# Modulation weights through a buffer and a queue of their own, and decay constants computed earlier, in a two-block decoder kernel

## The chip, the cores and the metric

The kernel runs on one core of a Trainium2 chip, as one launch. The metric is the device time of that launch in microseconds. Three runs of the kernel before took 985.2, 986.3 and 988.33 us; the median is 986.3 us. Engines are named as the profile names them: PE (matmul) with PEld (its weight loads), DVE, ACT, POOL (GpSimd) and SP, which issues most of the DMAs.

## The reference

There are 256 tokens of width 1024, all in float32. The first block mixes three attention branches (a low-rank attention with rotary positions, a dilated attention in three groups, and attention over 256 memory rows), gates each with a sigmoid of its own projection, adds them, and runs a convolutional feed-forward network of width 2816. The second block has two layers. Each layer modulates its input with a shift, a scale and a gate that depend on a condition vector `c`, and runs a gated linear recurrence beside a matrix-memory branch:

```
c_act = silu(c)
for l in range(2):
    mod = c_act @ w_ada[l] + b_ada[l]            # 1024 -> 3072
    shift, scale, gate = split(mod, 3)
    h = rms_norm(x, norm_g[l]) * (1 + scale) + shift
    ...                                          # h @ w_in, both branches, y = [..] @ w_out
    # in the recurrence: log_a = -8 * r * softplus(-lam)
    x = x + gate * y
```

The modulation depends on `c` alone, so it can be computed at any time before the second block. So can `softplus(-lam)`, which depends on a parameter alone.

## The kernel before

**Products.** Each float32 weight block of 128x1024 (512 KB) is fetched by SP into one of four buffers of the pool `raw`. ACT rounds it to `hi` (L254), DVE subtracts to get `lo` (L257), and PE forms three products for each pair (L266). The helper `load` does this for all weights, and `hi` and `lo` have four buffers each. A block that takes part in a product with 256 columns gives PE 24 matmuls. A `raw` buffer is free for the next fetch when its subtraction has ended, and SP issues in its own order, so a fetch that waits for a buffer holds back all that stand behind it.

**Modulation.** `w_ada` has 24 blocks of 128x1024 for each layer, 48 in all. A block is not multiplied on PE: DVE forms the dot product of each row with `c_act` in one pass (L504, a multiplication with an accumulator, in two records: the pass and the reading of the accumulator) and writes a column of `mod`. The generator `ada_blocks` yields after each block; `ada_steps(n)` takes n steps of it. In the kernel before, a step fetches a block through the same four `raw` buffers and the same SP queue (L503) and reduces it at once.

**The order.** The string `MIX` lists the steps of the mixing stage: `ls`, `lt`, `ly` are scores, transposes and sums of one head of the low-rank attention, `ds`, `dt`, `dy` those of the dilated one, `dp` a projection for it, `ga` to `gc` and `ba` to `bc` gates and branches, and `x1`, `x2`, `x3` are one, two or three modulation steps. There are 28 modulation steps in it, 9 more in the output projection and the feed-forward's down projection, and 13 in the first layer. From the program so recorded a scheduler sets the order of the instructions on each engine; what it builds is fixed then, and each engine runs its instructions in that order, waiting at each for its semaphores.

**Decay constants.** `csp` and `ncsp` (128x16) are computed by 2 activations on ACT and 25 short DVE operations and a memset (L987 to L1001), written in the program behind the feed-forward network.

**POOL** has little to do before: it adds in the feed-forward network (L948), issues nine DMAs, among them `ali` (768 KB, the bias of the dilated attention, twice) and `row` (512 KB, a gain spread over the partitions), and masks and adds in the second block.

Of the kernel before, what the change touches and what calls it, by code (L numbers as in the profile page):

```python
# [28 lines left out]
FENCE = 4  # L29
STREAM = 32  # L30
HOLD = 3
MIX = """gc0 lr ms0 gc1 ln ms1 mt0 gc2 my0 ms2 mt1 lq0 my1 lq1 ms3 mt2 lq2 my2 lq3 mt3 lk my3 lv gc3
    ls0 bc0 bc1 ls1 bc2 bc3 lt0 dp0 ly0 ls2 lt1 x1 dp1 ly1 ls3 lt2 x1 dp2 ly2 ls4 lt3 x1 dp3 ly3 ls5 lt4 x1 dp4 ly4 ls6 lt5 x1 dp5 ly5 ls7 lt6 x1 dp7 ly6 lt7 x1 ga0 ly7 x1 dp6 x1
    x1 ga1 x1 ga2 x1 ds0 ga3 ds1 ba0 ba1 ba2 ba3 dt0 dp8 dy0 dt1 dp9 dy1 x1 dp10 x2 dp11 x2 dp12 x2 dp13 x2 dp14 x3 ds2 dp15 x1
    ds3 gb0 x1 dt2 gb1 x1 dy2 x1 dt3 gb2 dy3 gb3 bb0 bb1 bb2 bb3"""
ADA_O = ((1,), (1,), (1,), ())
ADA_DOWN = ((1, 4), (3,), (1, 4), (1,))
ADA_RGZ = (1, 1, 1, 1)
# [159 lines left out]
def block_kernel(ctx: ExitStack, tc: tile.TileContext, T: dict, out: bass.AP):  # L198
    nc = tc.nc
    pe, act, dve, pool, dma = nc.tensor, nc.scalar, nc.vector, nc.gpsimd, nc.sync  # L200

    cp = ctx.enter_context(tc.tile_pool(name="cp", bufs=1))
    rawp = ctx.enter_context(tc.tile_pool(name="rawp", bufs=RAW))
# [7 lines left out]
    fill2 = ctx.enter_context(tc.tile_pool(name="fill2", bufs=1))  # L211
    dve.memset(fill2.tile([P, 48], F32, name="fill2"), 0.0)
# [10 lines left out]

    def slot(i, dt=F32, stream=False):
        a = STREAM if stream else 0
        return sp.tile([P, KT * S + 64], dt, name=f"s{i}", tag=f"s{i}")[:, a:a + KT * S].rearrange("p (k n) -> p k n", k=KT)
# [102 lines left out]
    def col(name, i=0, n=1):  # L329
        return cols[:, COL[name] + i:COL[name] + i + n]  # L330
# [19 lines left out]
    dve.memset(cp.tile([P, STREAM], F32, name="fill3"), 0.0)  # L350
# [11 lines left out]
    class Sums:  # L362
# [6 lines left out]
        def add(self, sq, k):  # L369

            if k < 6:
                g = k % 4
                pe.matmul(self.part[32 * g:32 * g + 32], lhsT=ones[:, :32], rhs=sq, start=k < 4, stop=k >= 2)
            if k == 5:
                part = one()
                act.copy(part, self.part)
                self.out = [sm_tile()[:, :P], sm_tile()[:, :P]]
                for t in range(2):
                    pe.matmul(self.out[t], lhsT=part[:, t * P:(t + 1) * P], rhs=ones32, start=True, stop=False)
# [118 lines left out]
    mod = cp.tile([P, 2, 24], F32, name="mod")  # L498

    def ada_blocks(l, c_act):  # L500
        for m in range(24):
            raw = rawp.tile([P, 1024], F32, name="raw", tag="raw")
            dma.dma_start(out=raw, in_=T[f"w_ada{l}"][m])  # L503
            dve.tensor_tensor_reduce(out=raw, in0=raw, in1=c_act, op0=ALU.mult, op1=ALU.add, scale=1.0,  # L504
                                     scalar=0.0, accum_out=mod[:, l, m:m + 1])
            yield
        dve.tensor_tensor(out=mod[:, l], in0=mod[:, l], in1=col("b_ada_2", 24 * l, 24), op=ALU.add)
        dve.scalar_tensor_tensor(out=mod[:, l, 8:16], in0=mod[:, l, 8:16], scalar=1.0, in1=col("norm_g_2", 8 * l, 8),
                                 op0=ALU.add, op1=ALU.mult)
        while True:  # L510
            yield
# [11 lines left out]


    with tc.tile_pool(name="l1", bufs=1) as l1, tc.tile_pool(name="pS", bufs=1) as pS:
        dve.memset(l1.tile([P, STREAM], F32, name="fill5"), 0.0)
        mask = l1.tile([P, S], F32, name="mask")
        yT = l1.tile([P, 8, S], F32R, name="y", tag="y")

# [62 lines left out]
        for quarter in (0.0, 0.25):  # L592
# [4 lines left out]
            r = one()  # L597
# [33 lines left out]
        rs_kv = t2.tile([P, S], F32, name="rstd", tag="rstd", bufs=3)  # L631

        rcs = {}

# [173 lines left out]
        def merge_branch(name, j, tg, first=False):  # L808
# [4 lines left out]
            else:  # L813
                t = two()
                dve.scalar_tensor_tensor(out=t, in0=tg[:, jj], scalar=1.0, in1=ps, op0=ALU.add, op1=ALU.mult)
                dve.tensor_tensor(out=merged[:, jj], in0=merged[:, jj], in1=t, op=ALU.add)


        sx, pts, yps, sets, tgs, ali = {}, {}, {}, {}, {}, {}
        for step in MIX.split():  # L820
            n, i = step.rstrip("0123456789"), int(step.lstrip("abcdefghijklmnopqrstuvwxyz_") or 0)
            if n == "ms":
                sx[n, i] = mem_scores(i)
            elif n == "mt":
                pts[n, i] = transposed(sx["ms", i], [0, S, P, S + P])
            elif n == "lt":
                pts[n, i] = transposed(sx["ls", i], [S, 0, P])
            elif n == "dt":
                pts[n, i] = transposed(sx["ds", i], [768, 896, 1024, 0, 128, 256, 384, 512, 640])
            elif n == "my":  # L830
                mem_sums(i, pts["mt", i])
            elif n == "lr":
                mla_sums_of_squares()
            elif n == "ln":
                mla_norms()
            elif n == "lq":
                mla_q(i)
            elif n == "lk":
                mla_k()
            elif n == "lv":  # L840
                mla_v()
            elif n == "ls":
                sx[n, i] = mla_scores(i)
            elif n == "ly":
                if i % 2 == 0:
                    yps[i // 2] = sm_tile()
                mla_sums(i, pts["lt", i], yps[i // 2])
            elif n == "dp":
                p = i // 8
                if i % 8 == 0:  # L850
                    sets[p] = [slot(x) for x in ((6, 4, 5), (0, 1, 2))[p]]
                dil_proj(p, i % 8, sets[p])
            elif n == "ds":
                if i % 2 == 0:
                    ali[i // 2] = dil_bias(i // 2)
                sx[n, i] = dil_scores(i % 2, sets[i // 2], ali[i // 2])
            elif n == "dy":
                dil_sums(i // 2, i % 2, sets[i // 2], pts["dt", i])
            elif n in ("ga", "gb", "gc"):
                if i == 0:  # L860
# [117 lines left out]

    for l in range(2):
        pool.dma_start(out=wif[:, l], in_=T[f"w_if{l}"])  # L980


    lam = col("rg_lambda_2", 0, 16)
    csp = l2.tile([P, 16], F32, name="csp")
    ncsp = l2.tile([P, 16], F32, name="ncsp")
    e, f, z2, w = (l2.tile([P, 16], F32, name=n) for n in ("sp_e", "sp_f", "sp_z", "sp_w"))
    act.activation(e, lam, AF.Abs)  # L987
    act.activation(e, e, AF.Exp, scale=-1.0)
    dve.tensor_scalar(out=f, in0=e, scalar1=2.0, scalar2=None, op0=ALU.add)
    dve.reciprocal(f, f)  # L990
    dve.tensor_tensor(out=f, in0=e, in1=f, op=ALU.mult)
    dve.tensor_tensor(out=z2, in0=f, in1=f, op=ALU.mult)
    dve.memset(w, 1.0 / 17.0)
    for k in (15, 13, 11, 9, 7, 5, 3, 1):
        dve.tensor_tensor(out=w, in0=w, in1=z2, op=ALU.mult)
        dve.tensor_scalar(out=w, in0=w, scalar1=1.0 / k, scalar2=None, op0=ALU.add)
    dve.tensor_tensor(out=w, in0=w, in1=f, op=ALU.mult)
    dve.tensor_scalar(out=e, in0=lam, scalar1=-1.0, scalar2=0.0, op0=ALU.mult, op1=ALU.max)
    dve.scalar_tensor_tensor(out=csp, in0=w, scalar=2.0, in1=e, op0=ALU.mult, op1=ALU.add)
    dve.tensor_scalar(out=csp, in0=csp, scalar1=4.0, scalar2=None, op0=ALU.mult)  # L1000
    dve.tensor_scalar(out=ncsp, in0=csp, scalar1=-1.0, scalar2=None, op0=ALU.mult)  # L1001

    def conv4(dst, ps, l, wname, bname, j):
        for m in range(2):
# [351 lines left out]
```

## Time and profile before

| | |
|---|---|
| median of 3 runs | 986.3 us |
| the profiled execution: its time, its span | 987.47 us, 985.8 us |
| busy: PE, DVE, ACT, POOL | 953.3, 735.2, 626.7, 53.8 us |
| mean clock granted to PE, as a share of full speed | 0.995 |
| weights fetched by SP | 185.17 MB |
| DMAs of POOL | 4.33 MB |
| modulation blocks | 48 of 512 KB, 59.3 us of DVE |

A matmul's end is modelled, so PE's busy time holds its short stalls only where they are longer than the pipeline is deep. Idle time before an instruction is shown in brackets with what ended it. The sum of a prediction is made against the span and its 987.47 us; the median lies 1.2 us lower.

### The profile page before, as it was taken

The numbers are of one execution on the slowest core, as the hardware profiler recorded it, in microseconds if no ns is written. First come the engines' busy times: TensorE is split into PE (matmuls) and PEld (weight loads), VectorE is DVE, ScalarE is ACT, GpSimd is POOL, SyncE is SP. The second block draws the span as 40 slices with busy tenths as digits, with TensorE's granted clock in tenths as the row PEclk, the third lists the DMA queues.
The fourth block names the chain that finished last, engine by engine and source line by source line (L and its number), as shares of the span: only waits on it lengthen the run. The fifth ranks groups of instructions, "written<-read, shape, count | busy, mean of one in ns | idle before, by whom it ended". The sixth has DMA issues, their size and how long they took to land.

```text
span 985.8 us, 19651 instructions
## 1 busy us (share of the span) xinstructions
PE 953.3 (97%) x7880; PEld 916.2 (93%) x7880; DVE 735.2 (75%) x1281; ACT 626.7 (64%) x1042; POOL 53.8 (5%) x61
## 2 busy tenths in 40 slices
PE   7999999999999999999989999999999999999997
PEld 5999999899989989999989899898999998899997
DVE  5856766567565888888856788589986798687754
ACT  7666555454345578887744776895645677886643
POOL 0000000000000002111200000000001000000021
PEclk9999999999999999999999999999999999999999
DMA  8654576777786766565667365355786464345552
GB/s 300 212 177 129 176 230 209 249 235 225 250 252 205 224 194 205 183 197 186 204 219 240 126 210 163 120 170 162 250 268 219 131 209 152 108 128 193 172 177 80
DMA packets 53371, 190.74 MB, mean 193 GB/s; under 512 B 6080, under 2 KB 6464, under 8 KB 53280
## 3 DMA queue, kind: packets, MB, share of 16 engines
q1 hardware_dynamic: 52272, 185.17, 58.0%
q0 software_dynamic: 1008, 4.33, 1.4%
q8 instruction: 61, 1.00, 0.4%
q14 instruction: 30, 0.25, 0.1%
HBM read 188.42 MB, written 1.05 MB: 192 GB/s over the span
## 4 chain that ended last, share of the span: by engine, by line
PE 66%; DVE 12%; ACT 10%; DMA 7%; issue 4%; POOL 0%; DVEq 0%; SPq 0%; ACTq 0%; POOLq 0%
PE mm L266 56%; DVE lo L257 5%; DMA raw<-in_w_ada 5%; ACT hi L254 3%; ACT fz L945 2%; ACT fw L946 2%; DVE fu L939 1%; PE sm L1051 1%; ACT s L491 1%; DMA raw<-in_w_dv 1%; DVE raw L504 1%; PE sm L1256 1%; PE sm L1207 1%; PE sm L669 1%; DMA raw<-in_w_mlx 1%
## 5 line engine op out<-in xcount | busy, mean ns | idle before, releaser
L257 DVE TENSOR_TENSOR lo<-raw,hi 128x1024 fp32r<-128x1024 f32 (+2 forms) x300 | 369.6, 1244 | 95.6 <-ACT hi L254 93.8
L254 ACT CAST hi<-raw 128x1024 fp32r<-128x1024 f32 (+2 forms) x300 | 308.7, 1040 | 153.0 <-PE mm L266 80.1
L266 PE MATMUL mm<-H,hi 128*128 128x256 f32 x1456 | 236.9, 281 | 0.1
L266 PE MATMUL mm<-H,lo 128*128 128x256 f32 x1456 | 233.4, 278 | 1.4 <-DVE lo L257 1.4
L266 PE MATMUL mm<-L,hi 128*128 128x256 f32 x1456 | 234.2, 279 | 0.1
L266 PEld LDWEIGHTS mm<-H,hi 128*128 128x128 f32 x1456 | 197.6, 189 | 2.2 <-DVE s L1008 0.8
L266 PEld LDWEIGHTS mm<-H,lo 128*128 128x128 f32 x1456 | 197.6, 189 | 1.6 <-DVE lo L257 1.6
L266 PEld LDWEIGHTS mm<-L,hi 128*128 128x128 f32 x1456 | 197.7, 189 | 0.7 <-DVE L L1029 0.3
L266 PE MATMUL mm<-hi,s 128*128 128x256 f32 (+1 forms) x1032 | 148.0, 283 | 0.2 <-ACT s L494 0.2
L266 PEld LDWEIGHTS mm<-hi,s 128*128 128x128 f32 x1032 | 131.8, 189 | 1.9 <-ACT s L494 0.4
L504 DVE CUSTOM_DVE_ANT_0 raw<-raw,c_act 128x1024 f32<-128x1024 f32 x48 | 59.3, 1235 | 63.4 <-DMA raw<-in_w_ada 63.4
L266 PE MATMUL mm<-lo,s 128*128 128x256 f32 (+1 forms) x516 | 84.9, 284 | 5.7 <-DVE lo L257 5.7
L266 PEld LDWEIGHTS mm<-lo,s 128*128 128x128 f32 x516 | 70.5, 190 | 7.0 <-DVE lo L257 6.1
L266 PE MATMUL mm<-s,hi 128*128 128x256 f32 x320 | 53.5, 286 | 0.0
L266 PEld LDWEIGHTS mm<-s,hi 128*128 128x128 f32 x320 | 44.3, 190 | 6.3 <-PE mm L266 2.5
L438 ACT ACTIVATE sq<-xn 128x256 f32<-128x256 f32 (+1 forms) x28 | 14.3, 511 | 43.6 <-POOL xn L1320 32.6
L266 PE MATMUL mm<-s,lo 128*128 128x256 f32 x160 | 34.2, 281 | 0.0
L945 ACT ACTIVATE fz<-fu,cols 128x256 f32<-128x256 f32 x44 | 26.2, 595 | 7.6 <-DVE fu L939 7.6
L948 POOL TENSOR_TENSOR fz<-fz,fw 128x508 f32<-128x508 f32 x22 | 24.7, 1125 | 109.1 <-DVE fz L947 109.1
L491 ACT CAST s<-two 128x512 fp32r<-128x512 f32 x24 | 14.9, 619 | 22.7 <-DVE two L1261 22.7
L657 ACT ACTIVATE sx<-sx,nm 128x256 f32<-128x256 f32 (+3 forms) x24 | 13.3, 555 | 24.6 <-DVE nm L654 24.6
L266 PEld LDWEIGHTS mm<-s,lo 128*128 128x128 f32 x160 | 25.4, 189 | 2.0 <-issue 1.2
(320 smaller groups left out, 1152.1 us busy)
## 6 DMA issues: line engine op xcount, KB each, us to landing
raw<-in_w_ada SPq DMA_DIRECT2D x48, 512.0 KB, 4.5
raw<-in_w_up SPq DMA_DIRECT2D x44, 512.0 KB, 4.4
raw<-in_w_out SPq DMA_DIRECT2D x32, 512.0 KB, 4.3
raw<-in_w_down SPq DMA_DIRECT2D x20, 512.0 KB, 4.3
raw<-in_w_mlx SPq DMA_DIRECT2D x16, 512.0 KB, 4.3
raw<-in_w_rgx SPq DMA_DIRECT2D x16, 512.0 KB, 4.2
raw<-in_w_mlo SPq DMA_DIRECT2D x16, 512.0 KB, 3.8
raw<-in_w_rgz SPq DMA_DIRECT2D x16, 512.0 KB, 4.3
```

The lines of the kernel that those rows point to most:

```text
L254: act.copy(hi[:, :n], raw)
L257: dve.tensor_tensor(out=lo[:, :n], in0=raw, in1=hi[:, :n].bitcast(F32), op=ALU.subtract)
L266: pe.matmul(dst, lhsT=t[x], rhs=t[y], start=(first and i == 0), stop=(last and i == n - 1))
L438: return act.activation(sq[:, :src.shape[-1]], src, AF.Square, accum_out=acc)
L491: act.copy(hi, src)
L504: dve.tensor_tensor_reduce(out=raw, in0=raw, in1=c_act, op0=ALU.mult, op1=ALU.add, scale=1.0, scalar=0.0, accum_out=mod[:, l, m:m + 1])
L657: act.activation(sx[:, a:b], src, AF.Exp, bias=nm[:, i:i + 1], accum_out=den[:, i:i + 1])
L669: pe.transpose(ps[:, i * P:(i + 1) * P], sx[:, o:o + P], ident)
L939: dve.tensor_tensor(out=u, in0=ps, in1=rs.unsqueeze(1).to_broadcast([P, 2, S]), op=ALU.mult)
L945: act.activation(z[:, i], u[:, i], AF.Identity, scale=col("conv_w", 88 + c), bias=col("conv_b", c))
L946: act.activation(w[:, i], u[:, i], AF.Identity, scale=col("conv_w", c))
L948: pool.tensor_tensor(out=z[:, :, 2:], in0=z[:, :, 2:], in1=w[:, :, :S - 2], op=ALU.add)
```

## The change

Three things are changed. First, a modulation block gets a single buffer of its own (`rawa`, 4 KB on each partition), and its fetch is issued by POOL's queue. A step now reduces the block that the step before fetched, and then issues the next fetch. Second, the `x` steps in `MIX` stand one at a time, from the middle of the memory attention to the end; there are still 28, and the other 22 stay where they were. Third, the decay constants are computed in the mixing stage (`cs`). To make room, one kind of temporary has 5 buffers instead of 6, the kept reciprocal roots have one instead of 3, a constant of 1/32 is folded into a copy, and some fillers go.

```
-    ls0 bc0 bc1 ls1 bc2 bc3 lt0 dp0 ly0 ls2 lt1 x1 dp1 ly1 ls3 lt2 x1 dp2 ...
+    ls0 bc0 bc1 x1 ls1 bc2 bc3 x1 lt0 dp0 ly0 x1 ls2 lt1 dp1 ly1 x1 ls3 lt2 dp2 ...
...
     def one():
-        return t2.tile([P, S], F32, name="one", tag="one", bufs=6)
+        return t2.tile([P, S], F32, name="one", tag="one", bufs=5)
...
-                act.copy(part, self.part)
+                act.mul(part, self.part, 1.0 / 32.0)
...
     def kept(ps):
-        r = t2.tile([P, S], F32, name="rstd", tag="rstd", bufs=3)
+        r = t2.tile([P, S], F32, name="rstd", tag="rstd", bufs=1)
...
     def ada_blocks(l, c_act):
-        for m in range(24):
-            raw = rawp.tile([P, 1024], F32, name="raw", tag="raw")
-            dma.dma_start(out=raw, in_=T[f"w_ada{l}"][m])
-            dve.tensor_tensor_reduce(out=raw, in0=raw, in1=c_act, op0=ALU.mult, op1=ALU.add, scale=1.0,
-                                     scalar=0.0, accum_out=mod[:, l, m:m + 1])
-            yield
+        for m in range(25):
+            if m:
+                dve.tensor_tensor_reduce(out=raw, in0=raw, in1=c_act, op0=ALU.mult, op1=ALU.add, scale=1.0,
+                                         scalar=0.0, accum_out=mod[:, l, m - 1:m])
+            if m < 24:
+                raw = rawp.tile([P, 1024], F32, name="rawa", tag="rawa", bufs=1)
+                pool.dma_start(out=raw, in_=T[f"w_ada{l}"][m])
+                yield
...
+        def decays():
+            lam = col("rg_lambda_2", 0, 16)
+            t = one()
...
+            elif n == "cs":
+                decays()
...
-    act.activation(e, lam, AF.Abs)
-    act.activation(e, e, AF.Exp, scale=-1.0)
```

The scheduler's order follows the recorded program loosely. On POOL, from the start of the program to its first work for the feed-forward network, these DMAs stood before:

```order
L766 DMA s_2474<-in_ali 128x1536
L766 DMA s_3266<-in_ali 128x1536
L881 DMA row<-in_rows 128x1024
L962 DMA two<-in_sel 128x512
L881 DMA row<-in_rows 128x1024
```

Now, on the same engine and in the same place:

```order
L505 DMA rawa<-in_w_ada 128x1024 x29
L766 DMA s_2507<-in_ali 128x1536
L505 DMA rawa<-in_w_ada 128x1024 x6
L766 DMA s_3290<-in_ali 128x1536
L505 DMA rawa<-in_w_ada 128x1024 x13
L904 DMA row<-in_rows 128x1024
```

All 48 fetches stand on POOL ahead of the first `row`, that is in the mixing stage and the start of the output projection, although 22 of the steps are recorded later; the two `ali` fetches stand among them.

On DVE, around the end of the low-rank attention's last head (`sx` is that head's exponentials, `y` its result), before:

```order
L661 TENSOR_SCALAR sx<-sx,rd 128x128
L257 TENSOR_TENSOR lo<-raw,hi 128x1024 x2
L504 ISA raw,mod<-raw,c_act 128x1024
L504 ISA mod 128x1
L504 ISA raw,mod<-raw,c_act 128x1024
L504 ISA mod 128x1
L257 TENSOR_TENSOR lo<-raw,hi 128x1024 x2
L492 TENSOR_TENSOR y<-sm,y 128x256
L257 TENSOR_TENSOR lo<-raw,hi 128x1024
L504 ISA raw,mod<-raw,c_act 128x1024
```

And now:

```order
L661 TENSOR_SCALAR sx<-sx,rd 128x128
L501 ISA rawa,mod<-rawa,c_act 128x1024
L501 ISA mod 128x1
L255 TENSOR_TENSOR lo<-raw,hi 128x1024 x2
L501 ISA rawa,mod<-rawa,c_act 128x1024
L501 ISA mod 128x1
L255 TENSOR_TENSOR lo<-raw,hi 128x1024 x2
L489 TENSOR_TENSOR y<-sm,y 128x256
L501 ISA rawa,mod<-rawa,c_act 128x1024
L501 ISA mod 128x1
L255 TENSOR_TENSOR lo<-raw,hi 128x1024 x2
```

A reduction now stands after every one or two subtractions. Counted over the whole order of DVE, the 1st reduction stands behind 10 subtractions and the 48th behind 88; before, the 1st stood behind 36, the 27th behind 87 and the other 21 behind 97 to 226.

## Rows read from the trace of the kernel before

**Rows 1.** The page: engines' busy time, share of the span, count of instructions.

```profile
PE 953.3 (97%) x7880; PEld 916.2 (93%) x7880; DVE 735.2 (75%) x1281; ACT 626.7 (64%) x1042; POOL 53.8 (5%) x61
```

**Rows 2.** By stretch: busy of PE, PEld, DVE, ACT, POOL (count), PE clock, DMA share, GB/s.

```profile
100.00:184.00 84.00, 84.00 (x686) 80.61 (x685) 57.02 (x121) 44.41 (x82) 0.00 (x0) 1.00 0.64 204
220.00:300.00 80.00, 75.11 (x588) 71.08 (x587) 55.19 (x84) 30.82 (x44) 0.00 (x0) 1.00 0.76 243
...
490.00:512.00 22.00, 16.31 (x126) 15.91 (x125) 15.01 (x40) 11.35 (x19) 2.02 (x4) 0.92 0.68 223
```

**Rows 3.** Waits: who waited for whom, us in total, times, longest.

```profile
PE mm L266 <- DVE lo L257: 8.6, 4, 4.5
```

**Rows 4.** Timeline of PE, 255 to 302: start, us, what, idle before it.

```profile
263.06 0.73 PE L266 MATMUL mm<-H,lo 128*128 128x256 f32 x4 [1.44 <-DVE lo L257]
...
275.35 0.74 PE L266 MATMUL mm<-lo,H 128*128 128x512 f32 x2 [1.43 <-DVE lo L257]
...
293.49 0.62 PE L266 MATMUL mm<-H,lo 128*128 128x256 f32 x4
```

**Rows 5.** Timeline of PE, 484 to 512.

```profile
492.45 0.74 PE L266 MATMUL mm<-lo,s 128*128 128x256 f32 x4 [1.20 <-DVE lo L257]
...
499.83 1.07 PE L266 MATMUL mm<-hi,s 128*128 128x256 f32 x8
505.39 1.00 PE L266 MATMUL mm<-lo,s 128*128 128x256 f32 x4 [4.49 <-DVE lo L257]
506.20 1.91 PE L266 MATMUL mm<-hi,s 128*128 128x256 f32 x8
```

**Rows 6.** The chain that ended last, 485 to 512.

```profile
497.29 5.65 DMA raw<-in_w_ada
```

**Rows 7.** Groups by line, 490 to 512: count, busy us, mean ns, idle before.

```profile
L995 DVE TENSOR_TENSOR sp_w<-sp_w,sp_z 128x16 f32<-128x16 f32 x8 | 1.4, 174 | 0.2
L988 ACT ACT_TABLE_LOAD x1 | 1.3, 1283 | 0.0
```

**Rows 8.** Line L504, the reduction: shortest, median, longest ns.

```profile
L504 DVE CUSTOM_DVE_ANT_0 raw<-raw,c_act x48: 1212/1225/1803, 118.1 to 735.6; 128x1024 f32<-128x1024 f32 x48
```

**Rows 9.** Timeline of all engines, 258 to 302.

```profile
266.86 1.23 DVE L257 TENSOR_TENSOR lo<-raw,hi 128x1024 fp32r<-128x1024 f32 x1 [1.58 <-ACT hi L254]
...
268.12 6.39 SPq L503 DMA_DIRECT2D raw<-in_w_ada  x3
...
272.92 1.23 DVE L504 CUSTOM_DVE_ANT_0 raw<-raw,c_act 128x1024 f32<-128x1024 f32 x1 [3.00 <-DMA raw<-in_w_ada]
...
288.77 1.22 DVE L257 TENSOR_TENSOR lo<-raw,hi 128x1024 fp32r<-128x1024 f32 x1
```

**Rows 10.** The chain that ended last, by time: start, us, what.

```profile
268.12 4.67 DMA raw<-in_w_ada
```

**Rows 11.** DMAs issued at 180 to 195: rate, then KB and median us to landing.

```profile
DMA packets 1011, 3.96 MB, mean 264 GB/s; under 512 B 112, under 2 KB 112, under 8 KB 1010
...
s<-in_ali POOLq DMA_DIRECT2D x1, 768.0 KB, 6.6
```

**Rows 12.** DMAs issued at 214 to 226.

```profile
DMA packets 588, 2.42 MB, mean 202 GB/s; under 512 B 64, under 2 KB 64, under 8 KB 587
...
s<-in_ali POOLq DMA_DIRECT2D x1, 768.0 KB, 5.6
```

**Rows 13.** DMAs issued at 354 to 360.

```profile
row<-in_rows POOLq DMA_DIRECT2D x1, 512.0 KB, 3.9
```

**Rows 14.** DMAs issued at 330 to 338.

```profile
row<-in_rows POOLq DMA_DIRECT2D x1, 512.0 KB, 8.0
```

**Rows 15.** The page: modulation fetches of SP.

```profile
raw<-in_w_ada SPq DMA_DIRECT2D x48, 512.0 KB, 4.5
```

**Rows 16.** Timeline of DVE, 36 to 110 and 138 to 166.

```profile
46.45 0.29 DVE L601 TENSOR_SCALAR one<-one 128x256 f32<-128x256 f32 x1
...
146.76 0.55 DVE L661 TENSOR_SCALAR sx<-sx,rd 128x256 f32<-128x256 f32 x2
```

More of the change, by code (lines that the diff above doesn't have):

```diff
@@ L31 @@
 HOLD = 3
[L32 to L35, printed above, removed]
+MIX = """gc0 lr ms0 gc1 ln ms1 mt0 gc2 my0 ms2 mt1 lq0 x1 my1 lq1 ms3 mt2 lq2 x1 my2 lq3 mt3 lk my3 lv x1 gc3
+    ls0 bc0 bc1 x1 ls1 bc2 bc3 x1 lt0 dp0 ly0 x1 ls2 lt1 dp1 ly1 x1 ls3 lt2 dp2 ly2 x1 ls4 lt3 dp3 ly3 x1 ls5 lt4 dp4 ly4 x1 ls6 lt5 dp5 ly5 x1 ls7 lt6 dp7 ly6 x1 lt7 ga0 ly7 x1 dp6 x1
+    ga1 x1 ga2 x1 cs ds0 ga3 ds1 ba0 x1 ba1 ba2 x1 ba3 dt0 dp8 dy0 x1 dt1 dp9 dy1 x1 dp10 x1 dp11 x1 dp12 x1 dp13 x1 dp14 x1 ds2 dp15 x1
+    ds3 gb0 dt2 gb1 x1 dy2 dt3 gb2 x1 dy3 gb3 bb0 bb1 bb2 bb3"""
 ADA_O = ((1,), (1,), (1,), ())
@@ L225, in slot @@
         a = STREAM if stream else 0
-        return sp.tile([P, KT * S + 64], dt, name=f"s{i}", tag=f"s{i}")[:, a:a + KT * S].rearrange("p (k n) -> p k n", k=KT)
+        return sp.tile([P, KT * S + (64 if i < 8 else 0)], dt, name=f"s{i}", tag=f"s{i}")[:, a:a + KT * S].rearrange("p (k n) -> p k n", k=KT)
     def two():
@@ L348, in block_kernel @@
     half = cp.tile([P, 56], F32, name="half")
-    dve.memset(cp.tile([P, STREAM], F32, name="fill3"), 0.0)
+    csp = cp.tile([P, 16], F32, name="csp")
+    ncsp = cp.tile([P, 16], F32, name="ncsp")
     HT = [cp.tile([P, KT, S], F32R, name=n) for n in ("H", "L")]
@@ L375, in add @@
                 part = one()
-                act.copy(part, self.part)
+                act.mul(part, self.part, 1.0 / 32.0)
                 self.out = [sm_tile()[:, :P], sm_tile()[:, :P]]
                 for t in range(2):
-                    pe.matmul(self.out[t], lhsT=part[:, t * P:(t + 1) * P], rhs=ones32, start=True, stop=False)
+                    pe.matmul(self.out[t], lhsT=part[:, t * P:(t + 1) * P], rhs=ones, start=True, stop=False)
             if k >= 6:
@@ L525, in block_kernel @@
     with tc.tile_pool(name="l1", bufs=1) as l1, tc.tile_pool(name="pS", bufs=1) as pS:
-        dve.memset(l1.tile([P, STREAM], F32, name="fill5"), 0.0)
+        dve.memset(l1.tile([P, 16], F32, name="fill5"), 0.0)
         mask = l1.tile([P, S], F32, name="mask")
@@ L630, in block_kernel @@
         tq = l1.tile([P, S], F32, name="tq")
-        rs_kv = t2.tile([P, S], F32, name="rstd", tag="rstd", bufs=3)
+        rs_kv = t2.tile([P, S], F32, name="rstd", tag="rstd", bufs=1)
         rcs = {}
@@ L816, in merge_branch @@
                 dve.tensor_tensor(out=merged[:, jj], in0=merged[:, jj], in1=t, op=ALU.add)
+        def decays():
+            lam = col("rg_lambda_2", 0, 16)
+            t = one()
+            e, f, z2, w = (t[:, 16 * n:16 * n + 16] for n in range(4))
+            act.activation(e, lam, AF.Abs)
+            act.activation(e, e, AF.Exp, scale=-1.0)
+            dve.tensor_scalar(out=f, in0=e, scalar1=2.0, scalar2=None, op0=ALU.add)
+            dve.reciprocal(f, f)
+            dve.tensor_tensor(out=f, in0=e, in1=f, op=ALU.mult)
+            dve.tensor_tensor(out=z2, in0=f, in1=f, op=ALU.mult)
+            dve.memset(w, 1.0 / 17.0)
+            for k in (15, 13, 11, 9, 7, 5, 3, 1):
+                dve.tensor_tensor(out=w, in0=w, in1=z2, op=ALU.mult)
+                dve.tensor_scalar(out=w, in0=w, scalar1=1.0 / k, scalar2=None, op0=ALU.add)
+            dve.tensor_tensor(out=w, in0=w, in1=f, op=ALU.mult)
+            dve.tensor_scalar(out=e, in0=lam, scalar1=-1.0, scalar2=0.0, op0=ALU.mult, op1=ALU.max)
+            dve.scalar_tensor_tensor(out=csp, in0=w, scalar=2.0, in1=e, op0=ALU.mult, op1=ALU.add)
+            dve.tensor_scalar(out=csp, in0=csp, scalar1=4.0, scalar2=None, op0=ALU.mult)
+            dve.tensor_scalar(out=ncsp, in0=csp, scalar1=-1.0, scalar2=None, op0=ALU.mult)
         sx, pts, yps, sets, tgs, ali = {}, {}, {}, {}, {}, {}
@@ L980, in block_kernel @@
         pool.dma_start(out=wif[:, l], in_=T[f"w_if{l}"])
[L983 to L986, printed above, removed]
-    act.activation(e, lam, AF.Abs)
-    act.activation(e, e, AF.Exp, scale=-1.0)
[L989 to L1001, printed above, removed]
     def conv4(dst, ps, l, wname, bname, j):
```

4 lines of the change are left out of this document (removed).

## The prediction

> **What bounds the kernel now.** I read the page first. PE is busy for 953.3 of 985.8 us [rows 1], so all that can be won by better fetching is what PE idles or runs at a lower clock. The stretches come second: PE idles for no time at 100 to 184, for 4.9 of 80 us at 220 to 300, and for 5.7 of 22 us at 490 to 512, where the granted clock is 0.92 [rows 2]. Third, the waits: four times PE waits for a subtraction on DVE, 8.6 us in all [rows 3], at 263, 275, 492 and 505 [rows 4, 5]. At the one at 505, SP issues a modulation fetch at 497.29 that lands after 5.65 us [rows 6]; its reduction stands on DVE ahead of the subtraction that PE wants. So a modulation block that arrives late stops PE through DVE's order. This is the mechanism that the change should relieve, and it is also the one by which it can hurt.
>
> **The change part by part.**
>
> *The modulation chain (added).* One buffer, a reduction that must follow the landing, and a fetch that must follow the reduction make one serial chain of 48 round trips. POOL's order shows all 48 ahead of the first `row`, and DVE's order puts the 48th reduction behind only 88 subtractions, so the chain has to run while PE does the products of those 88 blocks. I price one round trip, then the time that the order gives it.
>
> A round trip has four parts. The reduction takes 1.23 us [rows 8]. From DVE's end to an issue take 0.03 us: a subtraction from 266.86 that takes 1.23 ends at 268.09, and SP issues at 268.12 [rows 9]. From landing to DVE take 0.13 us: 268.12 plus 4.67 is 272.79, and the reduction starts at 272.92 [rows 9, 10]. The fourth part is the landing of 512 KB on POOL's queue, counted from the issue, and no row shows it beside the weights of the mixing stage. The nearest rows are the two fetches of `ali` in that stage, 768 KB in 6.6 and 5.6 us [rows 11, 12]. Less the time that 256 KB take at the rates of those stretches (0.262 MB at 264 and 202 GB/s, 1.0 and 1.3 us), they give 5.6 and 4.3 us. From below there is a 512 KB fetch of POOL that landed in 3.9 us with little beside it [rows 13]; from above the larger fetch itself, 6.6 us, and far off a 512 KB one that took 8.0 us [rows 14]. SP's own 48 take 4.5 us [rows 15]. I take the mean of 5.6 and 4.3, which is 4.9 us. The round trip is then 1.23 + 0.03 + 4.9 + 0.13 = 6.29 us.
>
> What the order gives: the second reduction stands behind the operation that starts at 46.45 us for 0.29 us [rows 16], so it can start at 46.7. The first starts about 9 us earlier and needs no more than that. The 48th stands ahead of the 89th subtraction, at 288.77 [rows 9], whose `lo` PE takes at 293.49 [rows 4]. With 46 round trips between the second and the 48th, the 48th starts at 46.7 + 46 x 6.29 = 336.0. Its own 1.23 us and a subtraction of 1.15 (two follow each other by that) bring the 89th `lo` to 338.4, against 293.5 before. **The stage ends 44.9 us later.** The kernel breaks even here at a round trip of 5.31 us, a landing of 3.92. Nothing hides the difference: PE takes `lo` in order and has only four buffers of it, 96 matmuls, ahead.
>
> Queued behind each waiting reduction on DVE are the subtractions of the next weights, the row maxima and the normalising of the scores. PE waits for all of them, and SP waits too, since a `raw` buffer is free only when its subtraction has ended; so weights cannot run ahead to make it good. On POOL, the two fetches of `ali` wait for a buffer that attention frees, and a modulation fetch stands behind each [the order on POOL above]; this can only lengthen two of the 46 links, by the 0.5 to 6 us of such a fetch, and I take none of it.
>
> *The modulation fetches of SP and their reductions (removed).* In the mixing stage the waits at 263 and 275 go, 2.9 us; they lie before 293.5, so the 44.9 us already holds them. Behind it, 21 blocks leave the later stages. The waits at 492 and 505 go, 1.20 + 4.49 = 5.7 us [rows 5]. After the second, eight matmuls take 1.91 us where eight took 1.07 just before [rows 5]; the granted clock falls to the lower of its two levels, 1.2 GHz, after PE has idled, and the stretch's clock of 0.92 over 22 us is 1.7 us of full speed lost [rows 2]. Together **7.4 us less**. What is late next there is the down projection's own loads, which have the four buffers for themselves; bounds 0 and 7.4.
>
> *The decay constants (moved).* 25 DVE operations of 0.17 us, 4.4 us, and one table load of 1.28 us [rows 7] move from 492 to 501 to the early mixing stage. They fall into DVE's waits for the chain, so they cost nothing; without that cover at most 4.4 us. The gain at the old place is in the 7.4.
>
> *Buffers and the folded 1/32.* No wait of PE in the rows goes back to a temporary or to a kept root; I take 0 for one buffer less of each kind, with bounds 0 and 2 us.
>
> The sum against the profiled execution: 987.5 + 44.9 - 7.4 = 1025.0. The median is 1.2 lower, so **1024 us**.
>
> **Two rules weighed.** The four fetches of POOL shown above, of 512 and 768 KB, take 3.9 to 8.0 us [rows 11 to 14]. The Trainium skill (DMA: Bandwidth & Descriptors, section Anatomy of one DMA — SWDGE (gpsimd) path) gives such a DMA about 2.0 us plus its bytes over 436 GB/s, an estimate of 3.2 us for 512 KB. By that rule a round trip would be 4.6 us, the chain would be done before PE needs it, and the result would be rival A. The trace does not agree: 768 KB would take 3.8 us by it and took 5.6 and 6.6 [rows 11, 12].
>
> DVE's normalising of scores, two in 0.55 us [rows 16], is the sort of instruction of which the Trainium skill (SBUF — State Buffer, section SBUF: two separate sides) says that it locks GpSimd out while it writes descriptors. By that rule a landing grows by half a microsecond at most here, and it points to rival B; no row tells it apart from other delays.
>
> **The rivals.**
>
> *A: the chain keeps up, and the kernel is faster.* If a fetch lands within 3.9 us, as the quiet one did [rows 13], a round trip is 5.3 us, the chain ends when PE needs it, the first term is zero, and the removed waits remain: 986.3 - 7.4 = 979 us. For it: the modulation blocks no longer fight for the four `raw` buffers, and SP's fetches have landed in 4.5 us with that fight. Against it: both `ali` rows. It decides below a landing of 3.9 us; at 4.1 the result is about 987, no change.
>
> *B: the landing is as long as the slower `ali`.* With 6.6 us a round trip is 7.99, the 48th reduction starts at 414, the stage is 123 us late: 986.3 + 123 - 7.4 = 1102 us. At 8.0 us it would be 1166. For it: two queues now share the DMA engines, and 21 more blocks come in this stage. Against it: 768 KB are half as much again, and a chain that holds SP back also empties the queues that it competes with.
>
> *C: the change does not do what it says.* The steps are recorded evenly, about 9 us apart, and could not stall if they ran so: the result would be A's 979. The built order excludes it, since it is fixed and has the reductions 5.3 us apart on average ((288.8 - 46.7) / 46); it gets no chance of its own.
>
> **How the numbers follow.** The forecast, with landings from 4.3 to 5.6 us, gives 996 to 1056 and has a chance of 0.66. Landings of 3.9 or less (A) have 0.12, between 3.9 and 4.3 0.09, above 5.6 (B) 0.13. The range of 8 in 10 takes landings from 4.1 to 5.7: 987 to 1061, and I set it at 988 to 1060. A measurement of this kernel can tell 0.3%, 3 us. Faster by more has 0.12; within it 0.05; slower 0.83, which is the forecast, B, and the upper part of the gap between A and the forecast.
>
> **What would show it.** In the new trace the largest wait of DVE should be L501 for `rawa`, over 40 times and some 1 to 4 us each; successive reductions should start 6 to 6.5 us apart; the landing of `rawa` should be near 4.9 us; PE should lose 45 us to waits for `lo` and for scores between 50 and 340 us, and little of its 5.7 us in the down projection. The forecast is wrong if the 48th reduction starts by 295 us, or if DVE waits for `rawa` and PE is still not held up.

## The result, and the profile after

The changed kernel takes 1000.8 us (997.4 to 1002.8, four runs) against 986.9 us for the kernel before beside it. The ratio is 1.0138, with a 95% interval of 1.0105 to 1.0171: it is 13.9 us slower. The profiled execution has a span of 998.7 us, 12.9 more than before.

The page of the changed kernel answers [rows 1]. PE is busy 5.5 us longer although it does the same matmuls, and POOL 24 us longer, which is the issuing of 48 DMAs:

```profile
PE 958.8 (96%) x7880; PEld 923.6 (92%) x7880; DVE 734.0 (73%) x1278; ACT 625.4 (63%) x1042; POOL 77.6 (8%) x109
```

The same three stretches as in [rows 2]:

```profile
100.00:184.00 84.00, 78.43 (x614) 75.22 (x613) 62.87 (x131) 40.63 (x81) 7.40 (x14) 0.96 0.70 229
220.00:300.00 80.00, 72.81 (x564) 71.07 (x565) 53.87 (x83) 31.37 (x45) 7.49 (x15) 0.96 0.71 238
490.00:512.00 22.00, 22.00 (x194) 22.00 (x192) 19.52 (x29) 17.72 (x33) 4.41 (x5) 1.00 0.55 180
```

At 100 to 184 PE did not idle before; now it idles for 5.6 us. At 220 to 300 it idles for 7.2 us instead of 4.9. In both stretches the granted clock is 0.96 instead of 1.00. At 490 to 512 the 5.7 us of idling are gone and the clock is full.

The waits, the modulation's and the largest of PE's in the mixing stage (who waited for whom: us in total, times, longest us):

```profile
POOL rawa L505 <- DVE mod L501: 188.8, 35, 8.7
...
DVE rawa L501 <- DMA rawa<-in_w_ada: 75.1, 40, 4.6
...
PE sm L669 <- DVE sx L661: 8.2, 5, 3.3
...
PE mm L264 <- DVE lo L255: 5.2, 2, 3.0
```

This is the loop of the prediction: POOL waits for the reduction, DVE for the landing, and PE for what stands behind the reduction on DVE. What PE waits for most is not `lo` but `sx`, the normalised scores. The line of the reduction (shortest, median, longest ns; first and last start), and the landings:

```profile
L501 DVE CUSTOM_DVE_ANT_0 rawa<-rawa,c_act x48: 1216/1225/1228, 40.9 to 321.7; 128x1024 f32<-128x1024 f32 x48
```

```profile
rawa<-in_w_ada POOLq DMA_DIRECT2D x48, 512.0 KB, 4.1
```

The median landing is 4.1 us, where 4.9 was forecast. One turn of the loop, with what it does to PE, on the timeline of all engines:

```profile
103.64 1.23 DVE L501 CUSTOM_DVE_ANT_0 rawa<-rawa,c_act 128x1024 f32<-128x1024 f32 x1 [0.61 <-DMA rawa<-in_w_ada]
...
105.17 0.53 POOL L505 DMA_DIRECT2D rawa<-in_w_ada  x1 [5.41 <-DVE mod L501]
...
109.19 1.23 DVE L501 CUSTOM_DVE_ANT_0 rawa<-rawa,c_act 128x1024 f32<-128x1024 f32 x1 [0.52 <-DMA rawa<-in_w_ada]
...
111.00 0.61 DVE L661 TENSOR_SCALAR sx<-sx,rd 128x256 f32<-128x256 f32 x2
...
111.41 1.16 PE L669 MATMUL sm<-cst,sx 128*128 128x128 f32 x4 [3.31 <-DVE sx L661]
```

The issue starts 1.53 us after the reduction's start (1.23 of work and 0.30 until POOL has it), the next reduction 4.02 us after that. `sx` stands behind it, and PE has idled for 3.31 us when it comes.

How late the program runs can be read from DMAs of POOL that stand at one place in both kernels. First before, the two `ali` and the first `row`, then after:

```profile
185.12 0.72 POOL L766 DMA_DIRECT2D s<-in_ali  x1 [184.60 <-ACT s L804]
...
218.14 0.53 POOL L766 DMA_DIRECT2D s<-in_ali  x1 [32.30 <-DVE nm L654]
...
332.46 0.53 POOL L881 DMA_DIRECT2D row<-in_rows  x1 [113.78 <-PE mm L266]
```

```profile
203.31 0.53 POOL L766 DMA_DIRECT2D s<-in_ali  x1
...
243.15 0.53 POOL L766 DMA_DIRECT2D s<-in_ali  x1 [4.26 <-DVE m L782]
...
354.65 0.53 POOL L904 DMA_DIRECT2D row<-in_rows  x1 [36.86 <-PE mm L264]
```

The changed kernel is 18.2, 25.0 and 22.2 us late at these places (an `ali` may itself stand behind a modulation fetch, by a few us). On PE, whose instructions stand in the same order in both kernels, it is 3.1 late already at 29 us, 27.9 at 260 and 22.0 at 300 (times of the kernel before); it keeps 22 through the feed-forward network (21.8 at 490) and wins 8 in the down projection, 7.4 of them by 512; 12.9 remain at the end.

### The profile page after: what moved, and what is told of

It is laid out like the page before. It is cut to its first block, busy times and chain, and to the rows that moved or that the text cites. A ratio compares the mean times of both kernels' runs of the same rounds, so it can differ in the third digit from the quotient of the medians.

```text
span 998.7 us, 19673 instructions
## 1 busy us (share of the span) xinstructions
PE 958.8 (96%) x7880; PEld 923.6 (92%) x7880; DVE 734.0 (73%) x1278; ACT 625.4 (63%) x1042; POOL 77.6 (8%) x109
## 4 chain that ended last, share of the span: by engine, by line
PE 71%; issue 18%; DMA 4%; DVE 3%; POOL 2%; ACT 1%; SPq 0%; POOLq 0%; DVEq 0%; ACTq 0%
PE mm L264 62%; DMA rawa<-in_w_ada 3%; POOL rawa L505 2%; PE sm L264 1%; PE sm L1053 1%; DVE lo L255 1%; DMA raw<-in_w_memkv 1%; PE sm L1209 1%; PE sm L1258 1%; PE sm L1249 0%; PE sm L453 0%; DVE rawa L501 0%; PE sm L994 0%; PE sm L1087 0%; PE sm L1251 0%
## 5 line engine op out<-in xcount | busy, mean ns | idle before, releaser
L255 DVE TENSOR_TENSOR lo<-raw,hi 128x1024 fp32r<-128x1024 f32 (+2 forms) x300 | 370.3, 1245 | 106.6 <-ACT hi L252 106.3
L501 DVE CUSTOM_DVE_ANT_0 rawa<-rawa,c_act 128x1024 f32<-128x1024 f32 x48 | 58.8, 1225 | 75.3 <-DMA rawa<-in_w_ada 75.1
L264 PE MATMUL mm<-s,hi 128*128 128x256 f32 x320 | 55.8, 294 | 1.1 <-ACT hi L252 1.1
L264 PEld LDWEIGHTS mm<-s,hi 128*128 128x128 f32 x320 | 46.4, 198 | 7.4 <-issue 2.9
L505 POOL DMA_DIRECT2D rawa<-in_w_ada x48 | 25.7, 535 | 286.3 <-DVE mod L501 188.8
```

The source lines that it names most:

```text
L255: dve.tensor_tensor(out=lo[:, :n], in0=raw, in1=hi[:, :n].bitcast(F32), op=ALU.subtract)
L264: pe.matmul(dst, lhsT=t[x], rhs=t[y], start=(first and i == 0), stop=(last and i == n - 1))
L505: pool.dma_start(out=raw, in_=T[f"w_ada{l}"][m])
```

## The experiments

T1 is the theory of the prediction: one buffer makes a serial chain, DVE waits in it in its order, and PE waits for what stands behind. The kernel before was measured again beside each four runs: 983.9 us for e1 to e4, 985.4 for e5 to e8, 984.6 for e9 to e12, 985.7 for e13 to e16. A ratio is always to that.

### e1: a short fetch

```
+BEHIND = [10, 14, 16, ... 86, 88]       # subtractions ahead of each reduction, as in the changed kernel
-pool.dma_start(out=raw, in_=T[f"w_ada{l}"][m])
+pool.dma_start(out=raw[:, :128], in_=T[f"w_ada{l}"][m][:, :128])
```

> Only the first 128 of a modulation block's 1024 columns are fetched (64 KB in place of 512); the rest of the sums is left out. The 48 reductions keep their full length and their places among the subtractions. Theory T1 (DVE waits in order for a serial chain of round trips through one buffer, and PE for the subtractions behind it): of the changed kernel's 1000.8 us the 20 that it loses between 50 and 240 us go, about 981 (977 to 985), and DVE's waits for rawa, 75 us in the trace, fall below 15. Rival T2 (21 more reductions, 26 us of DVE, stand between the subtractions of this stage): 1000, plus or minus 4, with PE's waits as they were. Rival T3 (10.5 MB more traffic in this stage): as T1 here.

972.8 us, ratio 0.988 (0.985 to 0.991). DVE's wait for `rawa` is 15.7 us. 28 us go (25 by the ratios), 8 more than T1 said; 3 of them are the start, which is 0.4 us late instead of 3.1. The buffer lies in another pool here, and the feed-forward network's matmuls take 281 ns instead of 276, which costs this run some 4 us. T2 (the work of 21 more reductions in this stage) falls: the work is all there.

### e2: two buffers

```
-raw = rawp.tile([P, 1024], F32, name="rawa", tag="rawa", bufs=1)
+raw = rawp.tile([P, 1024], F32, name="rawa", tag="rawa", bufs=2)   # room: 2 temporaries, fillers
```

> Two buffers rawa in place of one, so that a fetch runs while the block before it is waited for and reduced; all 48 blocks are fetched in full and the reductions keep their places. The room comes from two temporaries (3 instead of 5) and fillers. T1: the chain has about half its length per block, its waits go: 983 us (978 to 990, the upper end if the lost temporaries cost something). T2 (work of DVE) and T3 (traffic): 1000, plus or minus 4. Not to be told apart here: T2 from T3; the short fetch does that.

1000.0 us, ratio 1.015 (1.012 to 1.018): a miss for T1 by the end's time, but not by the trace. At the first `row` the kernel is 4.4 us late instead of 22.2, and PE does not idle from 50 to 300 us. It then loses steadily, without a wait, in matmuls that take longer. e5, e6 and e15 are about that.

### e3 and e4: reductions held back, and a late start

```
+with tc.issue_after(last_lo[0]):          # e3, e4: behind the subtraction recorded before it
     dve.tensor_tensor_reduce(out=raw, in0=raw, in1=c_act, ...)
...
+if m == 0 and l == 0:                      # e4 only: the first fetch waits for this
+    with tc.issue_after(last_lo[0]):
+        dve.memset(raw[:, :1], 0.0)
```

> One buffer and POOL's queue as in the changed kernel, but each reduction is held behind the subtraction recorded before it, so that none is drawn forward: the 28th stands behind 100 subtractions instead of 54, the 48th behind 230 instead of 88. T1: 28 reductions in the mixing stage are some 9 us apart, more than a round trip of 5.5 to 5.9; no chain stall there; 983 us (978 to 989; the upper end if the 13 reductions of the second block, two subtractions apart, wait). If the loss comes from the single buffer and the queue as such, wherever the reductions stand, or from the smaller number of temporaries: 998 to 1003.

> As the paced version, and the first modulation fetch waits for a one-column write of DVE that stands behind the 25th to 27th subtraction, instead of being issued at 1.3 us among the first weights. If that fetch takes the 3.1 us that the changed kernel is late at 30 to 40 us, this is 3 us (2 to 4) faster than the paced version. If the late start comes from elsewhere (order of the first loads, casts), they are equal within 1 us.

e3 takes 981.1 us, ratio 0.995 (0.993 to 0.998), e4 978.2, ratio 0.993 (0.990 to 0.996). With one buffer and POOL's queue kept, the places alone take away 18 to 20 us and make the kernel faster than before (20 of the 48 reductions stand behind the mixing stage again, as before the change; that their work or their traffic in the stage is not what costs, e1 and e5 show). The 3.0 us between e3 and e4 are what was said, though their intervals overlap; the traces agree, with a start that is 2.4 us later than before in e3 and 0.1 earlier in e4. In e4 T1 can be seen at another place, between the two layers (timeline of all engines):

```profile
727.25 0.57 POOL L511 DMA_DIRECT2D rawa<-in_w_ada  x1 [3.48 <-DVE mod L504]
...
732.54 1.23 DVE L504 CUSTOM_DVE_ANT_0 rawa<-rawa,c_act 128x1024 f32<-128x1024 f32 x1 [2.72 <-DMA rawa<-in_w_ada]
...
734.96 0.42 ACT L437 ACTIVATE sq<-xn 128x256 f32<-128x256 f32 x1 [6.58 <-POOL xn L1328]
```

### e5: two buffers, addresses kept

```
+rawq = ctx.enter_context(tc.tile_pool(name="rawq", bufs=1))        # behind all other pools
-raw = rawp.tile([P, 1024], F32, name="rawa", tag="rawa", bufs=1)
+raw = (rawp, rawq)[m % 2].tile([P, 1024], F32, name="rawa", tag="rawa", bufs=1)   # room: 3 temporaries
```

> Two buffers again, the reductions at the same places, but the second buffer is put behind all other pools, so that weights, hi, lo and the long-lived tiles keep their addresses in SBUF (in the first version of this experiment all behind the weight buffers moved by 4 KB, its matmuls in the feed-forward network took 283 ns instead of 276 and its subtractions 1222 ns instead of 1465, with no wait of PE). T1 (chain of round trips through one buffer) with the addresses as the reason why the first version won nothing at the end: 276 ns again, no chain stall, 983 us (979 to 988). If a second buffer does not help whatever the addresses: 998 to 1002.

978.1 us, ratio 0.994 (0.991 to 0.996), a little below the expected range. All 48 reductions stand where they stood in the changed kernel, and all bytes are fetched; 22.7 us go, and with them T3 (traffic). The line of the reduction with its idle time, and the two stretches:

```profile
L506 DVE CUSTOM_DVE_ANT_0 rawa<-rawa,c_act 128x1024 f32<-128x1024 f32 x48 | 58.3, 1215 | 1.3 <-DMA rawa<-in_w_ada 1.3
```

```profile
100.00:184.00 84.00, 84.00 (x686) 80.77 (x685) 66.58 (x142) 45.09 (x86) 8.97 (x17) 1.00 0.79 257
220.00:300.00 80.00, 80.00 (x642) 77.72 (x641) 58.27 (x92) 39.06 (x60) 6.34 (x12) 1.00 0.75 253
```

DVE waits for `rawa` 1.3 us instead of 75.1, PE idles in neither stretch, and more bytes per second move than before. The last reduction starts at 289.9 us instead of 321.7.

### e6, e9 and e15: addresses

```
+dve.memset(rawp.tile([P, 1024], F32, name="hole", tag="hole", bufs=1)[:, :16], 0.0)   # e6; e9: P, 256
-return sp.tile([P, KT * S + (64 if i < 8 else 0)], ...)
+return sp.tile([P, KT * S + (16 if i < 8 else 0)], ...)            # e6; e9: 32
-return t2.tile([P, S], F32, name="one", tag="one", bufs=5)
+return t2.tile([P, S], F32, name="one", tag="one", bufs=3)         # e6 and e15
```

> The changed kernel with one buffer, as it is, but with the addresses of the first two-buffer version: 4 KB left unused behind the weight buffers, fewer fillers, 3 temporaries. If the addresses cost what the two-buffer version lost, the chain's stalls (20 us by 240 us) and slower matmuls (276 to 283 ns, about 9 us by the end) add up: 1008 us (1004 to 1013). If the addresses cost nothing: 1000 (997 to 1003).

> The changed kernel with the same instructions in the same order (one memset of 16 columns more), but 1 KB is left unused behind the weight buffers and taken from the fillers of eight long-lived tiles: hi, lo and those tiles move by up to 1 KB in SBUF. If the addresses are what cost 14 us in the run with moved addresses (1014.5 against 1000.8): slower than 1000.8 by some us, 1004 to 1014, with matmuls of over 280 ns in the feed-forward network. If it was the order of a few dozen instructions there or the smaller number of temporaries: 1000.8, plus or minus 3, and 276 ns.

> The changed kernel with three temporaries instead of five and nothing else changed: the same order, but for three memsets and moves, as the run with moved addresses (1014.5), at the old addresses of hi, lo and the long-lived tiles. If the addresses cost the 14 us: 1001 (998 to 1004) and matmuls of 276 ns in the feed-forward network. If the temporaries and the order do: 1014 (1010 to 1017), 283 ns.

e6 takes 1014.5 us (ratio 1.030, 1.028 to 1.032), e9 998.1 (1.014, 1.010 to 1.017), e15 998.4 (1.014, 1.011 to 1.016). e15 has the order of e6 but for three entries on DVE, and the old addresses: so the 16 us between them are the addresses, not the temporaries. A move by 1 KB (e9) costs nothing, one by 4 KB with another spacing of eight tiles and of what lies in them (e6) does; which of its parts it is was not tried. The feed-forward network at 400 to 470 us in e6, and in e15 (groups by line: count, busy us, mean ns, idle before):

```profile
L267 PE MATMUL mm<-H,lo 128*128 128x256 f32 x193 | 31.1, 283 | 0.0
...
L258 DVE TENSOR_TENSOR lo<-raw,hi 128x1024 fp32r<-128x1024 f32 x25 | 30.7, 1227 | 15.5 <-ACT hi L255 15.5
```

```profile
L255 DVE TENSOR_TENSOR lo<-raw,hi 128x1024 fp32r<-128x1024 f32 x26 | 38.1, 1466 | 8.1 <-ACT hi L252 8.1
...
L264 PE MATMUL mm<-H,lo 128*128 128x256 f32 x208 | 32.1, 276 | 0.0
```

Where matmuls are slower the subtractions are faster, and the other way round. e6 ends 1.5 us above the range that it was given (1004 to 1013): up to 355 us it is no later than e15, and behind that it falls some 17 us back, with no longer waits of PE, where 9 had been expected.

### e7: half a fetch

```
+pool.dma_start(out=raw[:, :512], in_=T[f"w_ada{l}"][m][:, :512])
```

> 512 of a modulation block's 1024 columns are fetched (256 KB), the rest of the sums is left out; reductions in full length and at the same places, addresses kept. T1 says that there is a threshold: a landing of about 3.0 us (4.1 less 1.1 for 256 KB) makes a round trip of 4.4, and the chain keeps up with PE: 977 us (974 to 982), nearly all of the 28 us that the 64 KB fetch won. If the cost goes with the bytes (traffic beside the weights, rival T3): about half of it, 986 (983 to 989).

979.7 us, ratio 0.994 (0.992 to 0.997): T1's threshold, not the cost by bytes. It is a threshold with a soft edge: the landing is 3.4 us, DVE still waits 50.6 us for `rawa`, and at the first `row` the kernel is 7 us later than e5.

### e8 and e11: can it be better?

```
+BEHIND = [27, 30, ... 165, 168, 172, 176, ... 220]                 # e8: e4, the last 13 spread out
+if m < 2 and l == 0:                                               # e11: e5 with a late start
+    with tc.issue_after(los[LATE]):                                 # LATE = 4; los: the subtractions in order
+        dve.memset(raw[:, :1], 0.0)
```

> The paced version with a late start, and the last 13 reductions, which stood two subtractions apart in the second block (pairs of 206 to 230), set to every fourth from 172 on. In the paced version the last two reductions, at 725.7 and 732.5 us, hold up the norm between the two layers by waits for their fetches, and PE idles for 5.3 of 40 us there. T1: that goes, 978 less 5 = 973 us (970 to 976). If it is something else that PE waits for there: 978 as before.

> Two buffers with addresses kept, and the first two modulation fetches held behind a one-column write of DVE that stands behind the 5th subtraction. T1 for the start: the 3 us that the kernel is late at 30 us go, as in the paced version, 975 (972 to 977) against 978.1 without it; this would be the fastest of all. If the fetches at 1.3 us are not what the start loses: 978.

e8 takes 977.3 us (0.991, 0.988 to 0.994), e11 976.2 (0.991, 0.989 to 0.992). e8 is no faster than e4 by a measurable amount. What e4 loses behind 640 us is won (of PE's waits for `hi`, `lo` and `diag` between the layers, 5.3 us, 0.3 are left), but from 331 to 638 us e8 falls 8.5 us back against e4; 4.6 of it in the feed-forward network, whose matmuls take 281 ns instead of 276. The rest wasn't followed up. e11 has the lowest time of all runs that fetch whole blocks: 2 us below e5, within the range said, though the two intervals overlap.

### e10 and e16: single parts on the kernel before

```
-    ... x1 ga2 x1 ds0 ...
+    ... x1 ga2 x1 cs ds0 ...                # e10: decays() there, its lines behind the feed-forward network go
```

> The kernel before with only the decay constants moved to the mixing stage; modulation as before. My prediction had 0 for the move itself (at most +4.4, 25 operations of 0.17 us at the new place) and put the 7.4 us gained around 490 to 512 down to the modulation blocks: then no change, 985 (984 to 988), and PE's wait at 505 stays. If the constants had their part in that stall (they stood on DVE between 492 and 501): up to 6 us faster, 979 to 983.

> The kernel before with the evenly spread steps alone: its four shared buffers, SP's queue, decay constants where they were. If the waits at 263 and 275 us come from the reductions crowded there (x2, x3), they go, with the lower clock behind them: 979 to 983. If they come from the shared buffers and the fetches in SP's order: 985 (983 to 988).

e10 takes 986.8 us (ratio 1.0024, 1.0007 to 1.0040): no gain, as the prediction had it. e16, the new `MIX` alone, takes 984.1 (0.999, 0.997 to 1.001): no measurable change, near the second expectation. At 250 to 300 PE idles no more, but at 100 to 150, where it did not, it now idles for 2.8 us, so neither reading has it whole.

PE's wait in the down projection, 4.49 us before [rows 5], in e10 and in e16:

```profile
508.98 0.74 PE L266 MATMUL mm<-lo,s 128*128 128x256 f32 x4 [3.00 <-DVE lo L257]
```

```profile
502.87 0.75 PE L266 MATMUL mm<-lo,s 128*128 128x256 f32 x4 [1.78 <-DVE lo L257]
```

In both the wait at 492 is gone and this one is shorter, so that PE wins 4.3 and 5.4 us between 490 and 512. In both it had lost as much just before, 4.7 and 4.3 us, in a feed-forward network with matmuls of 281 ns. Since e16 has the constants at their old place, the win is no sign of theirs.

### e12 to e14: the queue or the place

```
-pool.dma_start(out=raw, in_=T[f"w_ada{l}"][m])
+dma.dma_start(out=raw, in_=T[f"w_ada{l}"][m])                      # e12
+BEHIND = [10, 14, ... 51, 53, 54, 56, 58, 60, ... 88, 90]          # e13
+BEHIND = [10, 14, 16, 19, 21, 23, ... 90, 93, 94, 96]              # e14
```

> The changed kernel with its one buffer, but SP issues the modulation fetches, among the weights, instead of POOL. T1 (one buffer): SP's own landings were 4.5 us, so a round trip is 5.9 instead of 5.5; PE loses in the mixing stage as before or some more, and SP, which waits in order for the buffer, holds weights back; the first fetch stands behind the first weights, which gives 3 back: 1005 (997 to 1015). Rival (POOL's software queue is what is slow): the stalls go, 981 (978 to 986).

> The changed kernel, one buffer and POOL's queue, with the reductions at the places that they had in the run on SP's queue (27th behind 53 subtractions instead of 52, the last behind 90 instead of 88, the others between by 1 or 2). T1 (links against places): a later place gives PE's side up to two weights more, some 6.6 us at 3.3 us for each of 89 subtractions in 300 us; 994 us (991 to 997). If it is the queue that made the SP run faster, wherever the reductions stand: 1000.8 (998 to 1003).

> The changed kernel with the places stretched evenly, the 1st where it was, the last behind 96 subtractions instead of 88. T1: in the kernel before the 96th subtraction comes some 22 us later than the 88th or 89th, 0.48 us for each of 46 links, which takes up most of the 0.69 us by which a link (5.89 on the mean) exceeds what the unstalled order takes (5.20, the run with two buffers and addresses kept); of the 22 us that PE is late at 332 us 17 to 22 go: 982 us (978 to 988), with one buffer and POOL's queue. If the single buffer costs by itself: 995 or more.

e12 takes 986.1 us (1.001, 0.999 to 1.003): far below the first range and at the edge of the second, whose reason is missed, since the stalls do not go (DVE still waits 61.6 us for `rawa`). A link of the chain (start of a reduction to the start of the next, where the next waited) has a median of 5.72 us, against 5.71 on POOL's queue; on the mean it is 5.6 against 5.8. So POOL's queue is not slower in the median, and 0.2 us slower on the mean. In e12 the chain also starts 2.6 us earlier, and the scheduler put most of the reductions from the 27th on one or two subtractions later. e13 has these places on POOL's queue: 996.2 us (1.011, 1.009 to 1.013), less than the changed kernel by 5 us in the medians and 3 by the ratios, whose intervals overlap: the way that T1 said, but not shown. The rest of e12's 14.7 us no run takes apart: by its trace 2.6 are the start and 5.5 the links (5.77 on the mean of 46 instead of 5.89), and how much of the latter is the queue's stays open.

e14 takes 1004.2 us (1.020, 1.017 to 1.022), where I had said 982. Stretching helped in the middle: at 308 us the kernel is 12.7 late instead of 22.2. Then it loses 8 us in front of the output projection (DVE, and the longest of PE's waits):

```profile
331.59 1.23 DVE L505 CUSTOM_DVE_ANT_0 rawa<-rawa,c_act 128x1024 f32<-128x1024 f32 x1 [2.12 <-DMA rawa<-in_w_ada]
...
337.11 1.23 DVE L505 CUSTOM_DVE_ANT_0 rawa<-rawa,c_act 128x1024 f32<-128x1024 f32 x1 [2.82 <-DMA rawa<-in_w_ada]
...
342.64 1.22 DVE L505 CUSTOM_DVE_ANT_0 rawa<-rawa,c_act 128x1024 f32<-128x1024 f32 x1 [2.02 <-DMA rawa<-in_w_ada]
...
349.56 0.72 PE L267 MATMUL mm<-hi,s 128*128 128x256 f32 x2 [2.13 <-ACT s L494]
```

Three reductions that wait stand there, with one and two subtractions between them, in front of work that PE needs at once, and for which it has nothing in store. The sum over the links did not see that. Another 4 us go in the feed-forward network, whose matmuls take 281 ns in this run.

## Why the prediction was right in its direction and wrong in its size

**The mechanism.** The forecast was the serial chain through one buffer and DVE's order, slower by 38 us. The mechanism is shown, by e1, e3 and e5, which remove it in three ways (short landing, later places, second buffer) and end 20 to 28 us below the changed kernel (18 to 25 by the ratios). Rival A (the chain keeps up, 979 us) and rival B (1102 us) did not come. C was excluded rightly: 40 of 48 reductions wait.

**The step that failed: the first term, 44.9 us.** The kernel was 22.2 us late where this term was to be read. Its parts:

- *The link.* It was 6.29 us in the forecast and is 5.89 on the mean ((321.68 - 50.74) / 46). The landing was the mis-sized part: issue to next reduction took 4.18 us (median) where 4.9 + 0.13 was taken from the two `ali`; POOL's issue came 0.30 us behind the reduction, not 0.03, which gives some back, and so do the few links that did not wait. 46 times 0.40 is 18.4 us too much.
- *The start.* The second reduction started at 50.7, not 46.7: 4.0 too little. Nearly all of it is the first fetch, at 1.3 us among the first weights, which the prediction did not price: in e11, which holds it back, the second reduction starts at 46.85.
- *The need.* The prediction put the 89th subtraction of before at 288.77 and PE's use of it at 293.49. That was read wrongly. It is the 86th that stands there; the 89th is the first of these two, and PE first uses its `lo` at 308.92 (timeline of the kernel before):

```profile
302.75 2.35 DVE L257 TENSOR_TENSOR lo<-raw,hi 128x1024 fp32r<-128x1024 f32 x2
...
308.92 0.63 PE L266 MATMUL mm<-H,lo 128*128 128x256 f32 x4
```

  That is 15.4 us too much.
- *Between the 48th reduction and that subtraction* DVE now has 2.8 us of other work, 1.4 of them a wait for ACT (it ends at 322.9; the subtraction starts at 325.75).

So 44.9 - 18.4 + 4.0 - 15.4 + 2.8 = 17.9 us, and the matching `lo` is used 22.2 us late (at 331.12). The 4.3 us that are left do not come from the chain's end: that `lo` was ready at 326.97, and PE took it 4.1 us later. PE was later than that before, 27.9 us at 260. The matmuls that it did from 50 to 260 us in the kernel before take it 235.3 us now instead of 210.0 (first before, then after):

```profile
50.00:260.00 210.00, 210.00 (x1694) 203.27 (x1694) 138.24 (x254) 111.13 (x194) 1.25 (x2) 1.00 0.65 207
```

```profile
52.60:287.90 235.30, 216.77 (x1694) 208.39 (x1694) 165.99 (x325) 112.08 (x199) 21.97 (x42) 0.97 0.70 235
```

18.5 us of that are waits, 8.2 of them for `sx` and 5.2 for `lo`; the other 6.8 are longer work at a granted clock of 0.97. The prediction read the chain at its end only, against a product of weights, and it had no clock in this term. With the right landing and the right need, and read at the end only, it would have said about 18 us, and come near the measured 22.2 partly by luck.

The break-even too was moved: it had a landing of 3.9 us as harmless. e7, with 3.4, still has PE 7 us behind e5 at the first `row`, and 2 behind the kernel before.

**The second term, -7.4 us.** Measured: 21.8 late at 490 us, 14.4 at 512, so -7.4, and 12.9 at the end. The waits at 492 and 505 are gone as said [rows 5]. But the reason was half right. In e3 the later blocks are back in the down projection and behind it, and it wins 8 us there as well (5.8 us early at 483, 14.0 at 599). So it is not needed that a block leaves the stage; that it no longer takes a `raw` buffer and a place in SP's order would explain it, but no run has that change alone, and e10 and e16 win a part of it with the shared buffers.

**The terms taken as nothing.** Decay constants: right by e10's time. Temporaries: right (e15, 998.4 with two fewer still). Addresses in SBUF were not thought of; the changed kernel's matmuls in the feed-forward network happen to take 276 ns as before.

**What was to be seen.** Waits for `rawa` over 40 times of 1 to 4 us: 40 times, up to 4.6, but not DVE's largest sum, which is `lo` for `hi` with 106.3 us. Reductions 6 to 6.5 us apart: 5.9. The landing 4.9: 4.1. PE's 45 us of waits between 50 and 340 us: 18.5. The rule of the Trainium skill (DMA: Bandwidth & Descriptors, section Anatomy of one DMA — SWDGE (gpsimd) path), an estimate of 3.2 us, is below the measured 4.1 as 4.9 was above it; its result, rival A, did not come.

## What to carry to other kernels

Where a queue's transfer goes through one buffer, write down a link (work, issue, landing) and the time that the built order leaves for it, at several points and not at the last alone: what waits directly behind the waiting instruction costs in full, what has buffers ahead costs little. A second buffer, or places far enough apart in the engine's order (e3; the small stretch of e14 was not enough), removes such a chain: 978 and 981 us here on the idle queue, against 986.1 with one buffer and the old places, nearly, on the busy one (e12). Compare matmul times in a stage that a change doesn't touch before you explain its result.

## What the runs showed of the hardware that was not expected

- Landing on POOL's queue beside weights: 2.8 us for 64 KB (e1), 3.4 for 256 KB (e7), 4.1 for 512 KB. That is about 2.6 us and then some 350 GB/s, an estimate worked out from the first and the last. It holds for these loops alone: 512 KB took 3.9 to 4.1 in six runs with the reductions close together, 4.6 in e3 and e4, 4.9 with two buffers (e5). The same loop on SP's queue has links about as long (median 5.72 against 5.71 us).
- POOL starts an issue 0.30 us after the end of the DVE work that it waits for, SP in e12 0.04 (1.53 and 1.26 us from the reduction's start, which takes 1.22).
- The feed-forward network ran in one of two patterns at full clock (one profiled execution of each run): matmuls of 276 ns with subtractions of about 1460 ns, or of 281 to 283 ns with 1220 to 1255, which cost 4 to 7 us there. 283 ns stand in e2 and e6 alone, and e6 against e15 shows that their addresses cost time. But e8, e10, e12, e14 and e16 have 281 ns with weights, `hi` and `lo` at the addresses of runs with 276; e16 differs from the kernel before in `MIX` alone. So addresses aren't all of it, and what else sets it stays open.
